# Centring, squares and running sums beside the output projections of a two-layer decoder trunk: their order and their places

## The chip, the cores and the metric

The kernel runs on one core of one Trainium2 chip. The metric is the device time of one execution in microseconds (us). The kernel before took 2110.22 us, the median of 3 runs (2108.76 to 2110.62).

Names used throughout: PE is TensorE with its matmuls, PEld its weight loads, DVE is VectorE, ACT is ScalarE, POOL is GpSimd, SP is SyncE, which issues most DMAs. All operands are 32 bits wide; a matmul operand is split into a high part (a rounding cast, on ACT) and a low part (what the cast left, a subtraction on DVE), and three matmuls (high x high, low x high, high x low) make one product of near full precision.

## The reference, cut to what matters

Two layers over 512 tokens and a width of 2048. Layer 0 mixes by indexed sparse attention, layer 1 by stick-breaking attention; both end in an output projection, and then the same tail:

```python
y = (o * silu(g)) @ w_out                       # output projection, 2048 x 2048
x = layer_norm(DN_ALPHA * x + y, ln_g, ln_b)    # mean and variance over 2048
x = x + (p[i] @ w_ple[i]) * sigmoid(x @ w_ple_gate[i])
```

The kernel holds all activations transposed, as 16 tiles m0 to m15 of 128 features x 512 tokens. The layer norm needs, for each token, the sum and the sum of squares over all 16 tiles.

## The kernel before, in words

**The stream of products.** Everything that PE does is cut into chunks, kept in one list (`chunks`), and `run` issues them in order. A chunk has 512 KB of weights. For chunk c the list of steps issues, ahead of its matmuls: the split of the weights of chunk c+2 (`split_w`: cast wh on ACT, L302, and wl on DVE, L303; there are three buffers of each, so that the split of c+2 needs the end of chunk c-1), sums of two weight tiles on DVE (`add_plus`, L291), accumulating loads issued by POOL (`add_load`, L286) and loads issued by SP (L207, six chunks ahead). Behind the matmuls come the evacuations, whatever was attached to the chunk with `then`, and a `pop`.

**The output projection** (`mix_out`, once a layer). Eight chunks of plain products make m0 to m3 (matmuls over 512 columns, L121 to L123). Then `quads` makes m4 to m15, two at a time, by seven products of half size instead of eight (a Strassen-like scheme; sums and differences of the quarters of u and of the weights are formed beforehand): six sources, each with products P1 to P7. A product is 24 matmuls over 256 columns (L187). The order is P1, P7, P6, P2, P4, P5 for the first source, then for each further one P7, P1, P3 of the source before, P6, P2, P4, P5, and at the very end the last P3. Seven such products are called a period here. The steps of a period: during P5 DVE forms the sum of weights for the next P6 and during P3 that for P4 (L291). After P7, P1, P6 and P3 ACT copies a half result out of PSUM (L217, L221, L225, L250), after P2, P4 and P5 DVE adds two halves (L229, L239, L233; L247 for the last P3). After P4 and after P3 a result tile is complete and goes to `out_done`.

**The layer norm's sums.** `out_done` (L818 on DVE) adds alpha times the residual to a result. When m0 and m1 are there, `guess` makes a rough mean c by one matmul pair; the variance is computed from tiles from which c was subtracted. From then on each tile puts a `center(m)` in a queue (`defer`), and those of m0 to m3 are put there with a due number nine chunks later. `pop` takes one function off this queue if its due number is below the number of the running chunk; a chunk with `pops = 0` takes none. `center` issues four operations: the subtraction of c on DVE (L843), the square on ACT (L850), the add of the tile to a1 on DVE (L851) and the add of the square to a2 on POOL (L852); the first item writes a1 and a2 instead (L846, L847). In the quads, P7, P2 and P5 have `pops = 0`, so pops are at P1, P3, P6 and P4. What is left in the queue after the last product is taken by `finish`, ahead of the matmuls of the first chunk of the per-layer embedding (`ple_chunks`), but behind that chunk's split. After that chunk `ln_stats` has PE sum a1 and a2 over the partitions (L856, L857), and ACT and DVE form mean and variance.

**The forms of u.** `us_ahead(kc)` splits four tiles of u (L105 on ACT, L106 on DVE), which plain chunks (0, kc) and (1, kc) need. `u_sums(j)` forms two differences and two further sums of a pair of u tiles (L770 to L773 on DVE), then splits one of them (L105, L106). It is attached to plain chunks 0 to 6: pairs 0 to 5 to chunks 0 to 5, and pairs 6 and 7 to chunk 6. In layer 1 the last head's attention tail (`b_tail`) hangs on chunks 0 and 2; `us_ahead(2)` hangs on chunk 1 and `us_ahead(3)` on chunk 5, in both layers.

Each engine works off its instructions in the order in which these functions issue them, and waits at an instruction whose inputs are not there.

Of the kernel before, what the change touches and what calls it, by code (L numbers as in the profile page):

```python
# [9 lines left out]
AF = mybir.ActivationFunctionType  # L10
OP = mybir.AluOpType
# [5 lines left out]
KT = D // P  # L17
# [364 lines left out]
def body(tc, xt, pt, positions, lncols, freq, w_in, w_out, w_gate, w_ple, w_kv, w_v, w_q, out):  # L382
    nc = tc.nc
    with tc.tile_pool(name="const", bufs=1) as const, \
            tc.tile_pool(name="raw", bufs=RAW_BUFS) as raw, \
            tc.tile_pool(name="hl", bufs=HL_BUFS) as hl, \
            tc.tile_pool(name="t", bufs=T_BUFS) as tp, \
            tc.tile_pool(name="dram", bufs=1, space=bass.MemoryType.DRAM) as dram, \
            tc.tile_pool(name="psum", bufs=1, space=bass.MemoryType.PSUM) as psum, \
            tc.manual_schedule():  # L390
        k = Kernel(tc, (const, raw, hl, tp, psum, dram))
        _emit(k, xt, pt, positions, lncols, freq, w_in, w_out, w_gate, w_ple, w_kv, w_v, w_q, out)


def _emit(k, xt, pt, positions, lncols, freq, w_in, w_out, w_gate, w_ple, w_kv, w_v, w_q, out):
    nc, const = k.nc, k.const
# [347 lines left out]
    def load_p(layer):  # L744
        pb.clear()
        for f in range(2):
            pb.append(k.tt(s="pin"))
            nc.sync.dma_start(pb[f], pt[layer, f])

    def prep_p(layer):  # L750
        pT[layer] = [k.split(t) for t in pb]

    def us(m):
        if m not in uhl:
            uhl[m] = k.split(u[m][0])
        return uhl[m]

    def us_ahead(kc):
        for m in range(4 * kc, 4 * kc + 4):
            if m in u:  # L760
                us(m)
# [3 lines left out]
    def u_sums(j):  # L765

        us(2 * j), us(2 * j + 1)
        a, b = u[2 * j][0], u[2 * j + 1][0]
        lo, hi = slice(0, HALF), slice(HALF, T)
        nc.vector.tensor_tensor(b[:, hi], b[:, hi], a[:, hi], op=OP.subtract)  # L770
        nc.vector.tensor_tensor(a[:, hi], a[:, lo], a[:, hi], op=OP.subtract)
        nc.vector.scalar_tensor_tensor(a[:, lo], b[:, hi], -1.0, a[:, lo], op0=OP.mult, op1=OP.subtract)
        nc.vector.scalar_tensor_tensor(b[:, lo], a[:, lo], -1.0, b[:, lo], op0=OP.mult, op1=OP.subtract)  # L773
        u23[j] = k.split(a)
        u.pop(2 * j)

    def u_more(name, js):

        for j in js:
            b = u[2 * j + 1][0]  # L780
            if j not in u14:
                u14[j] = k.tt(F32R, "u14")
            t, c = uhl[2 * j][name == "S4"], slice(0, HALF) if name == "S4" else slice(HALF, T)
            nc.scalar.copy(t[:, HALF:], b[:, c])
            nc.vector.tensor_tensor(u14[j][:, c], b[:, c], t.bitcast(F32)[:, HALF:], op=OP.subtract)
            if name == "S4":
                u.pop(2 * j + 1)
# [14 lines left out]
    def u_drop(what):  # L802
        for j in range(KT // 2):
            if what == 0:
                u23.pop(j)
            else:
                uhl.pop(2 * j + (what == 1))
                if what == 2:
                    u14.pop(j)

    dT = {}
    ln = {}
# [3 lines left out]
    def out_done(m, ps, z=None, negated=False):  # L816
        z = k.tt(s="z") if z is None else z
        nc.vector.scalar_tensor_tensor(z, x1.pop(m), ALPHA, ps, op0=OP.mult,  # L818
                                       op1=OP.subtract if negated else OP.add)
        dT[m] = z  # L820
        if len(dT) == 1:
            ln.clear()
        if len(dT) <= 2:
            rough.append(k.tt(F32R, "rough"))
            nc.scalar.copy(rough[-1], z)
        if "c" in ln:
            k.defer(lambda: center(m))
        elif len(dT) == 2:
            k.soon(guess)

    def guess():
        c_ps = k.ps("s")
        for n in range(2):
            nc.tensor.matmul(c_ps, ones_c, rough[n], start=n == 0, stop=n == 1)
        rough.clear()
        ln["c"] = k.tt(s="lnc")
        nc.scalar.copy(ln["c"], c_ps)
        for m in list(dT):
            k.defer_by(9, lambda m=m: center(m))

    def center(m):
        d = dT[m]
        nc.vector.tensor_tensor(d, d, ln["c"], op=OP.subtract)  # L843
        if "a1" not in ln:
            ln["a1"], ln["a2"] = k.tt(s="a1"), k.tt(s="a2")
            nc.vector.tensor_copy(ln["a1"], d)  # L846
            nc.scalar.activation(ln["a2"], d, AF.Square)  # L847
        else:
            sq = k.tt(s="sq")
            nc.scalar.activation(sq, d, AF.Square)  # L850
            nc.vector.tensor_tensor(ln["a1"], ln["a1"], d, op=OP.add)  # L851
            nc.gpsimd.tensor_tensor(ln["a2"], ln["a2"], sq, op=OP.add)  # L852

    def ln_stats():
        m_ps, e_ps = k.ps("s"), k.ps("s")
# [91 lines left out]
    def mix_out(layer):  # L947
        order = [(0, kc) for kc in range(3)] + [(1, kc) for kc in range(3)] + [(0, 3), (1, 3)]
        outs = {}
        for n, (b, kc) in enumerate(order):  # L950
            if b not in outs:
                outs[b] = [Out(KT, lambda ps, m=2 * b + i: out_done(m, ps)) for i in range(2)]
            if n == 0 and layer == 0:
                k.chunks[-3].after = lambda: us_ahead(0)
                k.chunks[-2].after = lambda: us_ahead(1)
            ch = k.chunk4(w_out[layer], 4 * b + kc, kc, outs[b], us,
                          pre=finish if n == 6 and layer == 0 else None)
            k.chunks.append(ch)
            if n in (0, 2) and layer == 1:
                ch.then(lambda n=n: b_tail(HEADS - 1, n // 2))  # L960
            if n in (1, 5):
                ch.then(lambda n=n: us_ahead(2 if n == 1 else 3))
            if kc == 1:
                ch.then(lambda b=b: [x1_load(layer, 2 * b + i) for i in range(2)])
            ch.then(lambda n=n: [u_sums(j) for j in ((6, 7) if n == 6 else (n,) if n < 6 else ())])

        def done(n, which, t):
            out_done(2 * n + 4 + which, t, t, which == 1)

        qs = k.quads([((w_out[layer], 2 * b), (w_out[layer], 2 * b + 1)) for b in range(2, KT // 2)], u_form, done)  # L970
        for n, name in enumerate(("P1", "P7", "P6", "P2")):
            qs[0][name].then(lambda n=n: u_more("S1", (2 * n, 2 * n + 1)))
        for q, name, js in ((0, "P4", (0, 1, 2)), (0, "P5", (3, 4, 5)), (1, "P7", (6, 7))):
            qs[q][name].then(lambda js=js: u_more("S4", js))
        for q in qs:
            for name in ("P7", "P2", "P5"):
                q[name].pops = 0
        for n, q in enumerate(qs):
            q["P7"].then(lambda n=n: x1_load(layer, 2 * n + 4))
            q["P4"].then(lambda n=n: x1_load(layer, 2 * n + 5))  # L980
        last = qs[-1]
        last["P6"].then(lambda: (u_drop(0), load_p(layer)))
        last["P4"].then(lambda: (u_drop(1), prep_p(layer)))
        last["P3"].then(lambda: u_drop(2))

    def x1_load(layer, m):
        x1[m] = k.tt(s="x1")
        nc.sync.dma_start(x1[m], xd[m] if layer else xt[m])
# [48 lines left out]
    def gate_end(n):  # L1037
        for m in range(4 * n, 4 * n + 4):
            xn.pop(m)
        if n < 3:  # L1040
            x1_split(8 + 2 * n)
            x1_split(9 + 2 * n)

    mix_out(0)
    ple_chunks(0)
    gate_block(0, x1_fin)
# [56 lines left out]
    def b_tail(h, step):  # L1103
        a = att[100 + h]
        if h < 4:
            a["v"] = values(vb[0], h)
        tail(h, a)[step]()
        if step == 1:
            if h == 3:
                vb.clear()  # L1110
            if h < KEEP_U:
                k.soon(lambda: u_store(h))
# [13 lines left out]
    qs = k.quads([(where_b[a](ha), where_b[b](hb)) for a, ha, b, hb in plan_b], form, b_done)  # L1126
# [20 lines left out]
    def out_store(m, v):  # L1147
        for c in halves(m):
            nc.sync.dma_start(out[m, :, c], v[:, c])

    mix_out(1)
    ple_chunks(1)
    gate_block(1, out_fin)
# [74 lines left out]
```

## Time and profile before

| | |
|---|---|
| median of 3 runs | 2110.22 us (2108.76 to 2110.62) |
| the profiled execution | 2110.23 us, its span 2108.5 us |
| PE busy | 2083.4 us (99%) |
| PEld busy | 1885.3 us (89%) |
| DVE busy | 1468.8 us (70%) |
| ACT busy | 1029.7 us (49%) |
| POOL busy | 243.7 us (12%) |
| plain chunks and quads of layer 0's projection | to about 792 us of the span |
| the same of layer 1 | about 1732 to 1903 us |

A row of a timeline gives the start within the span and the duration (us), engine, line, operation, output and input tiles, and in brackets how long the engine stood before it and what it waited for. A row of the waits gives the total in us, how often, and the longest. Matmuls overlap: each shows a duration of 0.28 us while the next starts 0.12 us later.

### The profile page before, as it was taken

What the parts mean: (1) busy time and instruction counts of PE and PEld (TensorE: products, weight loads), DVE (VectorE), ACT (ScalarE), POOL (GpSimd) and SP (SyncE); (2) the same over time, 40 slices, a digit from 0 to 9 for tenths busy, and PEclk for the clock granted to TensorE, in tenths of its full rate; (3) what the DMA queues carried; (4) which work ended last, traced back from release to release, by engine and by line L of the source; (5) the groups of instructions that cost most, each with busy time, mean ns of one, the idle gap of its engine ahead of it and who ended that gap; (6) DMA issues with size and microseconds to landing.
All of it is one profiled execution on the core that took longest, in us unless ns stands there. A gap on an engine that the chain in (4) does not pass through costs nothing. (4 is left out here: it accounts for less than half of the span.)

```text
span 2108.5 us, 32807 instructions
## 1 busy us (share of the span) xinstructions
PE 2083.4 (99%) x13024; PEld 1885.3 (89%) x13024; DVE 1468.8 (70%) x2254; ACT 1029.7 (49%) x1645; POOL 243.7 (12%) x311
## 2 busy tenths in 40 slices
PE   9999999999999999999999999999999999999999
PEld 7987888888888997888899999999999998997887
DVE  5577966556578887635777777777777778888633
ACT  4564345445455446423545455545555554446421
POOL 5201000000000220000011111111111110220000
PEclk9999999999999999999999999999999999999999
DMA  6322322222233662433455554655654564563431
GB/s 245 100 100 81 100 81 80 72 79 70 81 110 106 167 187 87 145 110 126 114 132 136 142 157 126 154 147 140 153 158 126 140 216 135 151 186 100 140 120 40
DMA packets 81226, 265.62 MB, mean 126 GB/s; under 512 B 9264, under 2 KB 9520, under 8 KB 81072
## 3 DMA queue, kind: packets, MB, share of 16 engines
q1 hardware_dynamic: 68976, 219.48, 30.6%
q0 software_dynamic: 12096, 44.05, 12.2%
q8 instruction: 102, 1.67, 0.3%
q14 instruction: 52, 0.43, 0.1%
HBM read 251.43 MB, written 12.06 MB: 125 GB/s over the span
## 5 line engine op out<-in xcount | busy, mean ns | idle before, releaser
L303 DVE TENSOR_TENSOR wl<-raw,wh 128x1024 fp32r<-128x1024 f32 (+1 forms) x489 | 607.2, 1246 | 295.0 <-ACT wh L302 290.9
L302 ACT CAST wh<-raw 128x1024 fp32r<-128x1024 f32 (+1 forms) x489 | 509.8, 1048 | 284.2 <-PE g L122 146.2
L187 PE MATMUL g<-f,wh 128*128 128x256 f32 x3360 | 619.4, 284 | 0.0
L121 PE MATMUL g<-h,wh 128*128 128x512 f32 (+1 forms) x1424 | 552.4, 388 | 1.0 <-ACT h L105 1.0
L122 PE MATMUL g<-l,wh 128*128 128x512 f32 (+1 forms) x1424 | 548.0, 385 | 0.8 <-DVE l L106 0.8
L123 PE MATMUL g<-h,wl 128*128 128x512 f32 (+1 forms) x1424 | 547.8, 385 | 0.5 <-DVE wl L303 0.5
L187 PEld LDWEIGHTS g<-f,wh 128*128 128x128 f32 x3360 | 528.6, 192 | 0.8
L187 PE MATMUL g<-f,wl 128*128 128x256 f32 x1680 | 475.5, 283 | 2.2 <-DVE wl L303 2.2
L187 PEld LDWEIGHTS g<-f,wl 128*128 128x128 f32 x1680 | 322.0, 192 | 3.8 <-DVE wl L303 3.0
L121 PEld LDWEIGHTS g<-h,wh 128*128 128x128 f32 x1424 | 267.6, 188 | 55.6 <-issue 2.9
L123 PEld LDWEIGHTS g<-h,wl 128*128 128x128 f32 x1424 | 267.5, 188 | 51.9 <-DVE wl L303 1.0
L122 PEld LDWEIGHTS g<-l,wh 128*128 128x128 f32 x1424 | 267.6, 188 | 51.7 <-DVE l L106 1.2
L187 PE MATMUL g<-h,wl 128*128 128x256 f32 x576 | 164.5, 286 | 8.9 <-DVE wl L303 8.9
L187 PE MATMUL g<-h,wh 128*128 128x256 f32 x576 | 163.1, 283 | 0.0
L187 PE MATMUL g<-l,wh 128*128 128x256 f32 x576 | 161.3, 283 | 0.0
L187 PEld LDWEIGHTS g<-h,wl 128*128 128x128 f32 x576 | 110.4, 192 | 12.0 <-DVE wl L303 11.9
L286 POOL DMA_DIRECT2D raw<-in_w_q_dram x60 | 53.0, 1031 | 585.0 <-issue 241.0
L187 PEld LDWEIGHTS g<-h,wh 128*128 128x128 f32 x576 | 110.4, 192 | 0.3
L187 PEld LDWEIGHTS g<-l,wh 128*128 128x128 f32 x576 | 109.8, 192 | 0.0
L291 DVE TENSOR_TENSOR raw<-raw,raw 128x1024 f32<-128x1024 f32 x84 | 102.3, 1218 | 0.1
L650 ACT ACTIVATE pr<-pr,s 128x128 f32<-128x128 f32 (+1 forms) x64 | 36.1, 564 | 126.0 <-DVE s L649 125.7
L474 POOL TENSOR_TENSOR rb<-rb,sin 128x512 f32<-128x512 f32 (+2 forms) x29 | 35.9, 1240 | 470.2 <-ACT rb L472 292.1
(206 smaller groups left out, 2441.4 us busy)
## 6 DMA issues: line engine op xcount, KB each, us to landing
raw<-in_w_in_dram SPq DMA_DIRECT2D x97, 512.0 KB, 3.3
raw<-in_w_out_dram SPq DMA_DIRECT2D x64, 512.0 KB, 4.2
raw<-in_w_gate_dram SPq DMA_DIRECT2D x64, 512.0 KB, 3.5
raw<-in_w_q_dram SPq DMA_DIRECT2D x64, 512.0 KB, 5.2
raw<-in_w_q_dram POOLq DMA_DIRECT2D x60, 512.0 KB, 6.0
raw<-in_w_kv_dram SPq DMA_DIRECT2D x56, 512.0 KB, 4.1
raw<-in_w_out_dram POOLq DMA_DIRECT2D x24, 512.0 KB, 5.6
xin<-in_x_dram SPq DMA_DIRECT2D x16, 256.0 KB, 6.0
```

The lines of the kernel that those rows point to most:

```text
L121: nc.tensor.matmul(out, ah, bh, start=start, stop=False)
L122: nc.tensor.matmul(out, ah, bl, start=False, stop=False)
L123: nc.tensor.matmul(out, al, bh, start=False, stop=stop)
L187: nc.tensor.matmul(ps[:, :HALF], a, b, start=start and j == 0 and n == 0, stop=stop and j == KT // 2 - 1 and n == 2, skip_group_check=True)
L286: self.nc.gpsimd.dma_start(ch.raw, ch.add, accum_op=OP.add)
L291: self.nc.vector.tensor_tensor(ch.raw, ch.raw, ch.plus.raw, op=OP.add)
L302: nc.scalar.copy(ch.h[:, i:i + w], ch.raw[:, i:i + w])
L303: nc.vector.tensor_tensor(ch.l[:, i:i + w], ch.raw[:, i:i + w], ch.h.bitcast(F32)[:, i:i + w], op=OP.subtract)
L474: nc.gpsimd.tensor_tensor(b[:rows, col:], b[:rows, col:], sin[:rows, col:], op=OP.mult)
L650: nc.scalar.activation(pr[:, :n], pr[:, :n], AF.Exp, bias=mx, scale=1.0, accum_out=sm)
```

## The change

`center` issues only its subtraction, and ahead of it the square and the two adds of the item before (`add_squares`). The last result of the sixteen is not put in the queue: `out_done` takes whatever the queue holds, centres it, and adds its square to a2 on DVE instead of POOL. In the quads of all sources but the last, P2, P4, P5 and P3 have no pops, so that P7, P1 and P6 have one; the products of the last source all have one. In layer 1 `u_sums` is attached one chunk later, with pairs 3 and 4 together on chunk 4.

```diff
@@ out_done
-        if "c" in ln:
+        if len(dT) == KT:
+            k.pop(KT, True)
+            center(m)
+            add_squares(nc.vector)
+        elif "c" in ln:
             k.defer(lambda: center(m))
@@
+    squares = []
+
     def center(m):
-        d = dT[m]
-        nc.vector.tensor_tensor(d, d, ln["c"], op=OP.subtract)
-        if "a1" not in ln:
-            ln["a1"], ln["a2"] = k.tt(s="a1"), k.tt(s="a2")
-            nc.vector.tensor_copy(ln["a1"], d)
-            nc.scalar.activation(ln["a2"], d, AF.Square)
-        else:
-            sq = k.tt(s="sq")
-            nc.scalar.activation(sq, d, AF.Square)
-            nc.vector.tensor_tensor(ln["a1"], ln["a1"], d, op=OP.add)
-            nc.gpsimd.tensor_tensor(ln["a2"], ln["a2"], sq, op=OP.add)
+        add_squares()
+        nc.vector.tensor_tensor(dT[m], dT[m], ln["c"], op=OP.subtract)
+        squares.append(m)
+
+    def add_squares(eng=None):
+        while squares:
+            d = dT[squares.pop()]
+            if "a1" not in ln:
+                ln["a1"], ln["a2"] = k.tt(s="a1"), k.tt(s="a2")
+                nc.vector.tensor_copy(ln["a1"], d)
+                nc.scalar.activation(ln["a2"], d, AF.Square)
+            else:
+                sq = k.tt(s="sq")
+                nc.scalar.activation(sq, d, AF.Square)
+                nc.vector.tensor_tensor(ln["a1"], ln["a1"], d, op=OP.add)
+                (eng or nc.gpsimd).tensor_tensor(ln["a2"], ln["a2"], sq, op=OP.add)
@@ mix_out
+        sums = ({0: (0,), 1: (1,), 2: (2,), 3: (3,), 4: (4,), 5: (5,), 6: (6, 7)},
+                {1: (0,), 2: (1,), 3: (2,), 4: (3, 4), 5: (5,), 6: (6, 7)})
...
-            ch.then(lambda n=n: [u_sums(j) for j in ((6, 7) if n == 6 else (n,) if n < 6 else ())])
+            ch.then(lambda n=n: [u_sums(j) for j in sums[layer].get(n, ())])
...
-        for q in qs:
-            for name in ("P7", "P2", "P5"):
+        for q in qs[:-1]:
+            for name in ("P2", "P4", "P5", "P3"):
                 q[name].pops = 0
```

## Rows read from the trace of the kernel before

**Rows 1.** The page, busy time of the engines.
```profile
PE 2083.4 (99%) x13024; PEld 1885.3 (89%) x13024; DVE 1468.8 (70%) x2254; ACT 1029.7 (49%) x1645; POOL 243.7 (12%) x311
```
**Rows 2.** Waits of PE over the whole span: us, times, longest us.
```profile
PE g L187 <- DVE wl L303: 11.1, 18, 1.2
```
**Rows 3.** Waits of PE in 700 to 770, then in 1800 to 1915 us.
```profile
PE g L187 <- DVE wl L303: 4.2, 7, 1.2
...
PE g L187 <- DVE wl L303: 4.6, 7, 1.2
```
**Rows 4.** Stretches, PE alone: length, busy (matmuls), granted clock, DMA share, GB/s.
```profile
700.00:769.00 69.00, 64.75 (x525) 1.00 0.60 158
1500.00:1569.00 69.00, 69.00 (x569) 1.00 0.57 149
```
**Rows 5.** Timeline of DVE in layer 0's projection.
```profile
744.95 1.21 DVE L303 TENSOR_TENSOR wl<-raw,wh 128x1024 fp32r<-128x1024 f32 x1
746.09 0.41 DVE L239 TENSOR_TENSOR o<-o,g 128x256 f32<-128x256 f32 x1
746.53 0.69 DVE L818 SCALAR_TENSOR_TENSOR o<-x,o 128x512 f32<-128x512 f32 x1
747.14 0.68 DVE L843 TENSOR_TENSOR o<-o,lnc 128x512 f32<-128x512 f32 x1
747.86 0.69 DVE L851 TENSOR_TENSOR a<-a,o 128x512 f32<-128x512 f32 x1
749.54 1.55 DVE L303 TENSOR_TENSOR wl<-raw,wh 128x1024 fp32r<-128x1024 f32 x1 [0.99 <-ACT wh L302]
```
**Rows 6.** Timeline of ACT at the same place.
```profile
747.94 0.63 ACT L850 ACTIVATE sq<-o 128x512 f32<-128x512 f32 x1 [3.88 <-DVE o L843]
748.48 1.98 ACT L302 CAST wh<-raw 128x1024 fp32r<-128x1024 f32 x2
```
**Rows 7.** Timeline of PE at the same place.
```profile
750.49 0.28 PE L187 MATMUL g<-h,wh 128*128 128x256 f32 x1
751.15 0.38 PE L187 MATMUL g<-h,wl 128*128 128x256 f32 x1 [0.38 <-DVE wl L303]
```
**Rows 8.** The page, DMA issues: count, KB each, us to landing.
```profile
raw<-in_w_out_dram POOLq DMA_DIRECT2D x24, 512.0 KB, 5.6
```
**Rows 9.** Timeline of POOL, an add of a square in layer 1.
```profile
1812.94 1.30 POOL L852 TENSOR_TENSOR a<-a,sq 128x512 f32<-128x512 f32 x1 [16.27 <-issue]
```
**Rows 10.** Timeline of DVE at the same place.
```profile
1813.46 1.85 DVE L303 TENSOR_TENSOR wl<-raw,wh 128x1024 fp32r<-128x1024 f32 x1 [0.91 <-ACT wh L302]
```
**Rows 11.** Timeline of DVE at the end of layer 0's projection.
```profile
794.08 0.69 DVE L818 SCALAR_TENSOR_TENSOR o<-x,o 128x512 f32<-128x512 f32 x1
...
797.02 1.54 DVE L303 TENSOR_TENSOR wl<-raw,wh 128x1024 fp32r<-128x1024 f32 x1 [0.92 <-ACT wh L302]
```
**Rows 12.** Timeline of PE at the same place, with the statistics' matmuls.
```profile
797.30 0.39 PE L123 MATMUL g<-h,wl 128*128 128x512 f32 x1
800.03 1.37 PE L856 MATMUL s<-a,ones 128*128 128x512 f32 x2 [2.35 <-DVE a L851]
801.29 2.07 PE L857 MATMUL s<-a,ones 128*128 128x512 f32 x2
```
**Rows 13.** A stretch of the last period: PE, PEld, DVE, ACT, POOL busy (instructions), clock, DMA.
```profile
769.00:792.00 23.00, 23.00 (x194) 23.00 (x193) 18.42 (x22) 11.52 (x17) 3.47 (x3) 1.00 0.67 193
```
**Rows 14.** Timeline of PE, plain chunks 1 and 2 of layer 1's projection.
```profile
1737.63 0.39 PE L123 MATMUL g<-h,wl 128*128 128x512 f32 x1
1739.00 0.50 PE L121 MATMUL g<-h,wh 128*128 128x512 f32 x1 [0.98 <-ACT h L105]
1740.34 0.50 PE L122 MATMUL g<-l,wh 128*128 128x512 f32 x1 [0.84 <-DVE l L106]
```
**Rows 15.** Timeline of ACT at the same place, the cast within u_sums(0).
```profile
1736.86 0.62 ACT L105 CAST h<-u 128x512 fp32r<-128x512 f32 x1 [2.83 <-DVE u L772]
```
**Rows 16.** A stretch after the statistics of layer 0, columns as in rows 13.
```profile
802.00:804.00 2.00, 2.00 (x4) 1.00 (x3) 0.31 (x1) 1.99 (x3) 0.00 (x0) 0.50 0.04 8
```

## The prediction

> **What bounds the kernel now.** I read the page first: PE is busy for 2083.4 of 2108.5 us [rows 1], so all that an edit of the other engines can return is time in which PE stands. The list of PE's waits says for what [rows 2]: above all for the weights' low part wl (L303, on DVE), 18 times. Fourteen of the 18 lie in the two output projections, seven in each [rows 3]. The table of stretches gives the size: 69 us of the first projection hold 525 matmuls of L187, 69 us of the later stage, which has the same kind of products and no centring, hold 569 [rows 4]; the 44 that are missing are 5.3 us at the pitch of 0.12 us.
>
> The timelines of one stall show its cause. DVE centres a result (L843 at 747.14); ACT has stood 3.88 us for that centring, because its queue holds the square (L850 at 747.94) ahead of the next casts of weights (L302 at 748.48) [rows 5, 6]. DVE in turn stands 0.99 us for the cast, forms wl from 749.54 until 751.09, and PE, which took the product's first matmul at 750.49, goes on at 751.15 [rows 5, 7]. DVE and ACT wait for each other in turn.
>
> **The change, part by part.** A product is 24 matmuls at 0.12 us, 2.88 us on PE; a period of seven products is 20.16 us.
>
> *Squares and sums one item late.* Each item keeps its centring, square, a1 add and a2 add; only the last a2 add goes from POOL to DVE. At a pop ACT now squares a tile that was centred a pop before, so its casts no longer stand behind this pop's centring.
>
> *Pops moved.* Before, the pops that may centre lie at P1, P3, P6 and P4; after, at P7, P1 and P6, and in the last period at all seven. P3 and P4 already carry a result each (L818), and P3 a sum of weights. Counting the queue's due numbers by hand: m0 stays at P6 of the second period; then three items go per period (m1 to m9), while two are made. The last period gets m10 (P7), m11 (P1), m12 (P6), m13 (P2) and m14 (P5), then m15 directly; before, it had m12, m13, and m14 and m15 at its very end.
>
> What it is moved past: SP holds none of it. On POOL, the accumulating load for the next P7 is issued in P3; the add of P1's pop now ends some 2.5 us later than the add that stands there today, and the load with it. From issue it lands in 5.6 us [rows 8], just when the cast of P7 comes up, 3 us ahead of what PE needs, so I cost it at nothing; cover is gone if a landing takes over 9 us.
>
> Does DVE have room? Its pitches, start to start [rows 5]: 1.14 us for a 128x1024 operation, 0.44 for a 128x256, 0.61 to 0.72 for a 128x512; I take 0.61, as the two of a pop no longer hang on each other. A period has 7 splits and 2 weight sums (9 x 1.14 = 10.3), 3 small evacuations (1.3), 2 results (1.2) and 3 items (3 x 1.22 = 3.7): 16.5 us. To this comes a cost that hardly shows now. While POOL adds a square, DVE is slowed: wl took 1.55 us instead of 1.21 [rows 5], and where it lay 0.78 us under an add (which ended at 1814.24) 1.85, so 0.64 more [rows 9, 10]. Today DVE idles through the first part of an add; after the change it will work beneath all 1.30 us. Scaled, 0.64/0.78 x 1.30 = 1.07 us an item (an estimate; bounds 0.34, the common case of today, and 1.30, all of the add). Three items: 3.2, in sum 19.7 of 20.16. The Trainium skill, "SBUF — State Buffer", section "Who interferes with whom", says that a VectorE instruction with two SBUF inputs and a GpSimd instruction that reads SBUF contend, the one that comes second being blocked for the whole of the other; by that an item would cost DVE 1.30 and a period 20.4, just over PE's. The overlapped row agrees in kind, at 82% of it.
>
> The fit is tight, but a burst has room: a split is issued two products ahead, 5.76 us, of which cast and split need 2.3. Walking the period by these pitches, DVE is 0.7, 2.3, 2.5 and 2.5 us behind the end of P7, P1, P3 and P6; P2 and P4 have little beside one split and win it back, and every wl is there 2 us before its need. So I take all fourteen stalls as gone. Their price: 4.2 + 4.6 us of idle [rows 3], plus what each loses beside it, since a matmul's 0.28 us counts as busy while the pitch is 0.12 (0.66 from 750.49 to 751.15 instead of 0.12, with 0.38 called idle [rows 7]: 0.16, and some 0.1 in the restart): 8.8 + 14 x 0.26 = 12.4. The counted stretch gives 2 x 5.3 = 10.6. **I take 12.0**, nearer to the timelines, where each start is seen.
>
> *Last result direct.* Before, the last result (L818) begins at 794.08; an older item and a split (797.02) follow on DVE ahead of m15's centring. PE stands for 2.35 us until L856 at 800.03, and L857 comes at 801.29, with POOL's last add [rows 11, 12]. After, m15 goes ahead of that split, but DVE arrives later: three items more before it, 3 x 2.3 = 6.9 us, against the 4.6 of 23 us and what follows in which it stood idle [rows 13]. My walk: wl of the last product is ready 1.0 us before its need, that of the first embedding product 0.5; L818 of m15 ends near 797.3; m14's a1, m15's centring and its a1 take 1.9, so L856 starts near 799.3, and L857 near 800.1, since the a2 add on DVE ends at 800.0. **1.2 us a layer, 2.4 in all**; bounds 0 (DVE a microsecond later) and 4.7 (all of the wait in both). The split put behind m15 is for the third embedding product, more than 5 us off, and costs nothing.
>
> *Layer 1's sums one product back.* At the end of the second product PE goes from 1737.63 to 1739.00 and to 1740.34 where 0.23 each is the pitch, 2.25 us lost [rows 14]. It waits for a split of u that stands on ACT behind the cast of u_sums(0), which itself waited 2.83 us for DVE [rows 15]. Put behind the second product's splits, u_sums(0) lets these begin some 2.5 us sooner. Cover gone elsewhere: sums 3 and 4 now share a product, 5 us of DVE in 5.4, and us_ahead(3) comes 2.8 us nearer to its use, by my walk just in time. **2.2 us**, bounds 1.5 and 2.25.
>
> **Sum.** 12.0 + 2.4 + 2.2 = 16.6. The profiled execution took 2110.23 (span 2108.5 and 1.7 around it), the median is 2110.22. 2110.2 - 16.6 = **2093.6 us**. Not counted: from 802 to 804 the granted clock was 0.50, the lower level (1.2 GHz), after PE's idle 2.35 us [rows 12, 16], 1.0 us lost. I keep it, as PE still stands there, if less.
>
> **Rivals.**
> (a) *DVE fills up.* If an add costs it 1.3 to 1.6 us, a period needs 20.4 to 21.3, DVE falls back by up to 1.1 a period, and over the last periods wl is late again: the 2.4 at the end are lost, and 2 to 3 us a layer in stalls: near 2100. For: 19.7 is already 98% of PE's period. Against: the one row shows 82%, not all, of an overlap. 0.17.
> (b) *Slower: adds and DVE block each other.* POOL's adds now begin amid DVE's work in every period. The old period takes 20.16 and some 1.8 of stalls, 22.0. DVE exceeds it once an add costs (22.0 - 16.5)/3 = 1.8 us. At 2.6, twice an add, a period takes 24.3: 2.3 x 4 periods x 2 layers = 18 us lost, less 2.2 for the sums: about 2126. Against: no row shows over 0.82 of the overlap. 0.04.
> (c) *The end opens fully*: DVE is slowed less (0.34), PE hardly stands at L856, and the clock stays up: 2.3 + 1.0 more, 2090.3. 0.13.
> (d) *It does not do what it says*: DVE runs a product late, so the square still meets a centring not done, as P7 and P1 are only 2.88 us apart; the stalls stay, only the sums return: 2108. For: the walk has DVE 2.5 us late. 0.08.
>
> **How the numbers follow.** Forecast 0.58, (a) 0.17, (b) 0.04, (c) 0.13, (d) 0.08. A measurement of this kernel tells about 0.2% (4.2 us) from no change. Faster by more: forecast, (a) and (c), 0.88; the same: (d), 0.08; slower: (b), 0.04. The range takes in forecast, (a) and (c): its low end is 12.4 + 4.7 + 2.25 and the clock's 1.0 below, 20.4, so 2089.5 with the rounding; its high end is (a) with its larger stalls, 2102.
>
> **What would show it.** Right: PE's waits for wl fall from 18 to the four of the later stage; ACT's square no longer waits for DVE; wl under an add takes up to 2.2 us; a 69 us stretch of the projection holds some 569 matmuls; PE stands 1 to 2 us ahead of L856; no stall at layer 1's start. Wrong: stalls on wl in the last period (a), DVE without idle and PE waiting throughout (b), ACT's square still waiting for L843 (d).

## The result and the profile after

The changed kernel took 2094.5 us, the kernel before 2110.4 beside it: a ratio of 0.9924, 95% interval 0.9905 to 0.9944, so 16 us (12 to 20) faster. One of its four executions took 4157.84 us, twice the time of the others, and is left out as slow. A second set of runs gave 2094.18 us (five runs within 2094.02 and 2094.33) and 0.9922 (0.9909 to 0.9934). The forecast was 2093.6, the range 2089.5 to 2102.0. The profiled execution took 2094.14 us, with a span of 2092.4; the span before was 2108.5.

The page's line of busy times, to be held beside [rows 1]: PE did the same 13024 matmuls in a span that is 16.1 us shorter.

```profile
PE 2079.5 (99%) x13024; PEld 1884.9 (90%) x13024; DVE 1479.1 (71%) x2256; ACT 1026.6 (49%) x1645; POOL 245.1 (12%) x309
```

PE's waits over the whole span, beside [rows 2]. The waits for wl are five instead of 18. Four of the five lie in the later stage, outside the projections; the fifth is new, in the first product of layer 1's quads. New too is a small one for L247, DVE's evacuation of the last product.

```profile
PE s L867 <- DVE a L862: 3.4, 2, 1.7
PE g L187 <- DVE wl L303: 2.1, 5, 0.5
PE o L703 <- POOL ident L400: 1.4, 1, 1.4
PE g L123 <- DVE wl L303: 0.5, 1, 0.5
PE g L121 <- DVE o L247: 0.4, 2, 0.2
```

ACT's waits for the centring ahead of a square, over the whole span: two lines of the kernel before, then one of the changed kernel. 28 such waits are down to four, one in each last period and one ahead of the square of each m15.

```profile
ACT sq L850 <- DVE o L843: 51.1, 22, 3.9
ACT sq L850 <- DVE z L843: 14.1, 6, 3.6
```
```profile
ACT sq L861 <- DVE o L849: 11.7, 4, 4.0
```

Two stretches, all engines, columns as in [rows 13]. The first answers to [rows 4]: 577 matmuls in 69 us instead of 525, with DVE busy for 62.5 of them. The second is the last period, which begins 6 us earlier than before: DVE is busy for 21.7 of 23 us, where it was for 18.4 [rows 13].

```profile
700.00:769.00 69.00, 69.00 (x577) 69.00 (x576) 62.53 (x69) 33.79 (x48) 18.34 (x16) 1.00 0.63 168
763.00:786.00 23.00, 22.98 (x192) 22.78 (x191) 21.71 (x25) 11.45 (x17) 6.43 (x5) 1.00 0.57 171
```

The place that answers to [rows 5 to 7], on DVE, ACT and POOL in turn. The square (now L861) does not wait at all for DVE's centring (now L849), it only follows the copy of PE's result (L221, which stood 0.98 us for PE); the cast comes at 749.49, while DVE is still at the a1 add and the centring ahead of that cast's split. And POOL's add now lies over DVE's work: the centring at 749.82 takes 1.78 us instead of 0.68.

```profile
745.71 0.69 DVE L862 TENSOR_TENSOR a<-a,o 128x512 f32<-128x512 f32 x1
746.31 0.68 DVE L849 TENSOR_TENSOR o<-o,lnc 128x512 f32<-128x512 f32 x1
747.75 1.55 DVE L303 TENSOR_TENSOR wl<-raw,wh 128x1024 fp32r<-128x1024 f32 x1 [0.75 <-ACT wh L302]
749.22 0.68 DVE L862 TENSOR_TENSOR a<-a,o 128x512 f32<-128x512 f32 x1
749.82 1.78 DVE L849 TENSOR_TENSOR o<-o,lnc 128x512 f32<-128x512 f32 x1
```
```profile
748.69 0.38 ACT L221 COPY s<-g 128x256 f32<-128x256 f32 x1 [0.98 <-PE g L187]
748.96 0.64 ACT L861 ACTIVATE sq<-o 128x512 f32<-128x512 f32 x1
749.49 1.04 ACT L302 CAST wh<-raw 128x1024 fp32r<-128x1024 f32 x1
```
```profile
749.74 1.31 POOL L863 TENSOR_TENSOR a<-a,sq 128x512 f32<-128x512 f32 x1 [1.53 <-ACT sq L861]
```

The end of layer 0's projection on PE, beside [rows 12]: PE waits 0.21 us for L247, then 1.72 us ahead of the statistics (L867, L868), where it waited 2.35.

```profile
790.33 0.39 PE L123 MATMUL g<-h,wl 128*128 128x512 f32 x1
790.93 0.50 PE L121 MATMUL g<-h,wh 128*128 128x512 f32 x1 [0.21 <-DVE o L247]
...
792.19 0.40 PE L123 MATMUL g<-h,wl 128*128 128x512 f32 x1
794.31 1.10 PE L867 MATMUL s<-a,ones 128*128 128x512 f32 x2 [1.72 <-DVE a L862]
795.24 1.02 PE L868 MATMUL s<-a,ones 128*128 128x512 f32 x2
```

The same place on DVE, beside [rows 11]. The split that stood ahead of m15 is gone from there, but L247 comes 4 us behind the end of its product, since DVE is late, and L818 takes 1.32 us under POOL's add. Of the 4 us, 0.75 are DVE's wait for a cast. That cast stood on ACT behind a copy of the last source (L236), which had waited 4.80 us for DVE (last line): once, at the end, the two engines still wait for each other in turn.

```profile
788.99 1.55 DVE L303 TENSOR_TENSOR wl<-raw,wh 128x1024 fp32r<-128x1024 f32 x1 [0.75 <-ACT wh L302]
790.47 0.41 DVE L247 TENSOR_TENSOR o<-o,g 128x256 f32<-128x256 f32 x1
790.91 1.32 DVE L818 SCALAR_TENSOR_TENSOR o<-x,o 128x512 f32<-128x512 f32 x1
792.15 0.68 DVE L862 TENSOR_TENSOR a<-a,o 128x512 f32<-128x512 f32 x1
792.76 0.68 DVE L849 TENSOR_TENSOR o<-o,lnc 128x512 f32<-128x512 f32 x1
793.47 0.69 DVE L862 TENSOR_TENSOR a<-a,o 128x512 f32<-128x512 f32 x1
```
```profile
787.12 0.37 ACT L236 COPY o<-g 128x256 f32<-128x256 f32 x1 [4.80 <-DVE o L233]
```

Behind it the granted clock stays at 1.00, where it was 0.50 [rows 16]:

```profile
796.00:798.00 2.00, 2.00 (x10) 1.56 (x9) 0.29 (x1) 1.98 (x4) 0.00 (x0) 1.00 0.31 72
```

Since PE issues the same matmuls in the same order, the two timelines of PE can be laid side by side, matmul by matmul. Each line below is one of them; the difference of two lines is what the stretch between them won or lost.

| matmul | starts before | starts after | shift |
|---|---|---|---|
| layer 0, the first behind the seventh wait | 766.16 | 760.13 | -6.03 |
| layer 0, the last output of the first embedding product | 796.16 | 790.93 | -5.24 |
| layer 0, second statistics matmul | 801.29 | 795.24 | -6.05 |
| layer 0, third matmul after the statistics | 804.01 | 796.56 | -7.45 |
| layer 1, end of plain chunk 1 | 1737.63 | 1729.86 | -7.77 |
| layer 1, chunk 2, second matmul | 1740.34 | 1730.31 | -10.03 |
| layer 1, first product of the quads | 1781.19 | 1771.51 | -9.68 |
| layer 1, the first behind the seventh wait | 1876.93 | 1860.88 | -16.04 |
| layer 1, the last output of the first embedding product | 1906.92 | 1891.68 | -15.24 |
| layer 1, second statistics matmul | 1912.05 | 1895.99 | -16.05 |

Fourteen stalls: 6.03 + 6.36 = 12.4 us won. The last periods: 0.79 + 0.80 lost. The statistics: 0.81 + 0.81 won. The clock of layer 0: 1.40 won. The sums of layer 1: 2.26 won, 0.35 lost again at the first product. The rest, between the layers: 0.3.

### The profile page after: what moved, and what is told of

Read it like the earlier page. It is cut to its first block, busy times and chain, and to the rows that moved or that the text cites. A ratio compares the mean times of both kernels' runs of the same rounds, so it can differ in the third digit from the quotient of the medians.

```text
span 2092.4 us, 32803 instructions
## 1 busy us (share of the span) xinstructions
PE 2079.5 (99%) x13024; PEld 1884.9 (90%) x13024; DVE 1479.1 (71%) x2256; ACT 1026.6 (49%) x1645; POOL 245.1 (12%) x309
## 4 chain that ended last, share of the span: by engine, by line
PE 91%; DVE 4%; issue 3%; ACT 1%; POOL 0%; POOLq 0%; DVEq 0%; ACTq 0%
PE g L187 36%; PE g L121 16%; PE g L123 16%; PE g L122 16%; PE s L592 2%; PE o L122 1%; PE o L123 1%; DVE wl L303 1%; PE o L121 1%; PE s L121 1%; PE s L122 1%; PE s L123 1%; PE s L526 1%; ACT wh L302 1%; DVE a L862 0%
## 5 line engine op out<-in xcount | busy, mean ns | idle before, releaser
L187 PE MATMUL g<-f,wh 128*128 128x256 f32 x3360 | 619.4, 284 | 0.0
L187 PEld LDWEIGHTS g<-f,wh 128*128 128x128 f32 x3360 | 529.1, 192 | 0.8
L187 PE MATMUL g<-f,wl 128*128 128x256 f32 x1680 | 476.3, 284 | 1.9 <-DVE wl L303 1.9
L187 PEld LDWEIGHTS g<-f,wl 128*128 128x128 f32 x1680 | 322.5, 192 | 3.5 <-DVE wl L303 2.7
L187 PE MATMUL g<-h,wl 128*128 128x256 f32 x576 | 163.5, 284 | 0.2 <-DVE wl L303 0.2
L187 PE MATMUL g<-h,wh 128*128 128x256 f32 x576 | 163.3, 284 | 0.0
L187 PE MATMUL g<-l,wh 128*128 128x256 f32 x576 | 161.7, 284 | 0.0
L187 PEld LDWEIGHTS g<-h,wl 128*128 128x128 f32 x576 | 110.7, 192 | 0.7 <-DVE wl L303 0.6
L187 PEld LDWEIGHTS g<-h,wh 128*128 128x128 f32 x576 | 110.7, 192 | 0.1
L187 PEld LDWEIGHTS g<-l,wh 128*128 128x128 f32 x576 | 110.0, 192 | 0.0
L291 DVE TENSOR_TENSOR raw<-raw,raw 128x1024 f32<-128x1024 f32 x84 | 102.4, 1218 | 0.1
```

The source lines that it names most:

```text
L187: nc.tensor.matmul(ps[:, :HALF], a, b, start=start and j == 0 and n == 0, stop=stop and j == KT // 2 - 1 and n == 2, skip_group_check=True)
L291: self.nc.vector.tensor_tensor(ch.raw, ch.raw, ch.plus.raw, op=OP.add)
```

## The experiments

The theory that the result suggests: the stalls are ACT's and DVE's waiting for each other, and DVE's whole work in the last period, POOL's blocking with it, sets when the statistics begin. The rivals stand in each expectation.

**One item late, alone.** The changed kernel with the old pops, the old sums and the last item through the queue, its square issued behind `finish`:

```diff
-        for q in qs[:-1]:
-            for name in ("P2", "P4", "P5", "P3"):
+        for q in qs:
+            for name in ("P7", "P2", "P5"):
```

> Squares and sums one item late; pops, layer 1 sums and the way of the last result as in the kernel before. Theory A (the stalls come from the square that stands on ACT ahead of the casts and waits for this pop's centring): ACT's square waits for DVE almost nowhere, 0 to 4 of the 14 stalls on wl in the projections are left, the time falls by 9 to 12 us against the kernel before, to 2098 to 2101. Theory B (the stalls come from items put on P3 and P4, which already carry a result and a sum of weights, so that DVE itself is late): 10 or more of the 14 are left and the time falls by less than 3 us. Under both the 2.2 us at the start of layer 1 stay.

Measured: 2103.9 us, ratio 0.9975 (0.9965 to 0.9984). Neither theory's number: in the side-by-side, 4.1 of layer 0's 6.0 us come back and 4.4 of layer 1's 6.4, but three of the seven stalls of each layer are left, with waits of 0.3 to 0.5 us. The square still waits for DVE there, 1.59 us at 737.83, and the timeline of DVE says why: the item is put on P3, behind a weight sum (L291) and a result (L818) that an add of POOL (last line) stretches to 1.78 us, and the next pop's square meets a centring that is not done.

```profile
737.83 0.63 ACT L857 ACTIVATE sq<-o 128x512 f32<-128x512 f32 x1 [1.59 <-DVE o L845]
```
```profile
733.61 1.21 DVE L291 TENSOR_TENSOR raw<-raw,raw 128x1024 f32<-128x1024 f32 x1
734.75 1.78 DVE L818 SCALAR_TENSOR_TENSOR o<-x,o 128x512 f32<-128x512 f32 x1
736.45 0.68 DVE L858 TENSOR_TENSOR a<-a,o 128x512 f32<-128x512 f32 x1
737.05 0.68 DVE L845 TENSOR_TENSOR o<-o,lnc 128x512 f32<-128x512 f32 x1
```
```profile
733.70 2.28 POOL L859 TENSOR_TENSOR a<-a,sq 128x512 f32<-128x512 f32 x1 [0.27 <-ACT sq L857]
```

That is rival (d) of the prediction in part: it comes true, at other products than it named, as long as the pops stay where they were.

**Pops moved, alone.** The kernel before, with

```diff
-        for q in qs:
-            for name in ("P7", "P2", "P5"):
+        for q in qs[:-1]:
+            for name in ("P2", "P4", "P5", "P3"):
```

> Pops moved to P7, P1 and P6 (all seven in the last period); square behind its own centring, sums and last result as before. Theory A: the square still waits for its centring on ACT, 8 or more of the 14 stalls are left, the time falls by less than 5 us against the kernel before. Theory B: 0 to 4 of the 14 stalls are left and the time falls by 9 to 12 us. Walking one period by the row's pitches, P1's and P6's squares would each hold ACT about 1 us and yet every wl would be in time, which is theory B's result; the last period, with five items, would show stalls of its own.

Measured: 2108.5 us, ratio 0.9989 (0.9979 to 0.9998), hardly anything. Up to the sixth stall layer 0 wins 4.0 us, then gives 3.6 back: with five items in the last period the stalls come there. In 700 to 769 us PE waits twice for wl, 1.4 us in all, and in 769 to 800 us, by the waits of that stretch:

```profile
PE g L187 <- DVE wl L303: 1.7, 2, 1.0
PE s L856 <- DVE a L851: 1.6, 1, 1.6
PE g L121 <- DVE o L247: 0.5, 1, 0.5
```

By the time this is theory A's result; by the stalls up to the last period, where two of seven are left in each layer, it is nearer to theory B's.

By the medians the two parts are worth 5.3 and 0.8 us alone and, with the sums, 10.3 together (below), but these times mix levels of the clock. In the first experiment's profile the granted clock fell behind both layers' statistics, and no execution's mean clock was above 0.998; of the kernel before beside it, six executions of 25 have 0.998. Against those six (median 2112.2 us) the first experiment's six at 0.998 (median 2103.5) are 8.7 us faster, about what its stalls show (4.1 + 4.4). The pops with the mean clock at 1.000 (two executions, 2107.0, against 2109.1) are worth 2.1, the sums 2.0 (next experiment), and the kernel with all three at 0.999 (2098.9 against 2110.7) 11.8. So the late square is the dearest of the parts, and together they are worth no more than their sum. Light places keep DVE's lateness short enough that an item is centred when the next pop's square comes; the late square keeps ACT free. That is how the traces above read.

**Layer 1's sums, alone.** The kernel before, with the table of sums of the change:

```diff
-            ch.then(lambda n=n: [u_sums(j) for j in ((6, 7) if n == 6 else (n,) if n < 6 else ())])
+            ch.then(lambda n=n: [u_sums(j) for j in sums[layer].get(n, ())])
```

> Only the layer 1 sums one product back; all else as before. The step's own price by the two traces: 2.26 us won at the start of layer 1, 0.38 us given back as a stall on wl in the first product of the quads, so 1.9 us net: 2108.3 to 2108.6. If the 0.38 belongs to the centring and not to the sums, it is absent here and 2.2 to 2.3 us are won.

Measured: 2110.05 us, ratio 1.0000 (0.9990 to 1.0009), not the time that was expected. The side-by-side shows the step's price as expected: 2.26 us won, 0.39 lost at the first product, so that loss belongs to the sums and not to the centring. But it did not reach the end: in this execution the granted clock fell behind layer 1's statistics too, which it had not in the profile of the kernel before, and 1.6 us went there. Nine of the ten executions have a mean clock of 0.998 (median 2110.2); against the six of the kernel before at that clock (2112.2) the sums return 2.0 us. These are stretches of PE alone, columns as in [rows 4]:

```profile
1910.00:1912.00 2.00, 1.85 (x5) 0.90 0.53 207
1912.00:1914.00 2.00, 2.00 (x5) 0.50 0.00 0
1914.00:1916.00 2.00, 2.00 (x8) 0.74 0.00 0
```

**All but the direct last result.** The changed kernel, m15 through the queue and its add on POOL:

```diff
-        if len(dT) == KT:
-            k.pop(KT, True)
-            center(m)
-            add_squares(nc.vector)
-        elif "c" in ln:
+        if "c" in ln:
...
-            ch = Chunk(k.whole(w_ple[layer], c), mms, pre=finish if c == 0 else None)
+            ch = Chunk(k.whole(w_ple[layer], c), mms, pre=(lambda: (finish(), add_squares())) if c == 0 else None)
```

> The changed kernel, but the last result goes through the queue and is centred behind the first embedding product's split, its a2 add on POOL. If taking the last result directly is worth what the traces show of L856 and L857 (0.8 us a layer and the clock of layer 0, 1.4 us, that goes with the shorter wait), the time is 1.6 to 3.5 us above the changed kernel, 2096 to 2098, and PE stands over 2.3 us ahead of the statistics. Rival: the end is set by DVE's whole work in the last period, in whatever order, and the time stays within 0.5 us of the changed kernel's.

Measured: 2098.9 us, ratio 0.9945 (0.9931 to 0.9960), against 0.9922 for the changed kernel: 4.8 us by the spans (2097.2 against 2092.4), more than was expected, and the rival is out. The list of PE's waits has up to 3.0 us ahead of the statistics, more than in the kernel before, and layer 0's clock falls again. In layer 1, where it does not fall, the difference is 1.7 us:

```profile
PE s L863 <- DVE a L858: 6.1, 2, 3.0
```

**The direct last result, alone.** The kernel before, with these lines, where the second argument puts the last a2 add on DVE:

```diff
-        if "c" in ln:
+        if len(dT) == KT:
+            k.pop(KT, True)
+            center(m, nc.vector)
+        elif "c" in ln:
             k.defer(lambda: center(m))
```

> The kernel before with the last result centred directly and its square added on DVE, all else as before. Ahead of the statistics a split (1.5 us under POOL's add) and 0.9 us of waiting for its cast go: L856 comes 1.5 to 2.4 us sooner a layer, 3 to 5 us in all and up to 3 us more where the lower clock behind the wait is avoided: 2102 to 2106. If instead taking it directly is only worth something beside the five items of the moved last period, the time falls by less than 2 us.

Measured: 2104.35 us against 2110.29, ratio 0.9971 (0.9960 to 0.9983): 5.9 us. By the side-by-side 1.8 us a layer of it are won at the statistics, and 1.4 are layer 0's clock. By the list of PE's waits the one ahead of the statistics is down to 0.9 us, and all 18 for wl are still there; the clock stays up in the profiled execution.

```profile
PE g L187 <- DVE wl L303: 10.4, 18, 1.2
PE s L859 <- DVE a L854: 1.7, 2, 0.9
```

**The changed kernel again**, without an edit, as the measure for the next.

> The changed kernel once more, beside the three below on the same chip. By its first runs 2094 to 2095 us. Some executions may be about 1.5 us longer: in the kernel before and in three of the experiments the granted clock fell to the lower level behind the wait ahead of the statistics of one layer or of both, and their times lie in steps of that size.

Measured: 2094.18 us; no run above 2094.33, no step.

**All adds of squares on DVE.** They are made one pop after their square, so that DVE does not wait for ACT.

```diff
-    squares = []
+    squares, sums_due = [], []
...
     def add_squares(eng=None):
+        while sums_due:
+            nc.vector.tensor_tensor(ln["a2"], ln["a2"], sums_due.pop(), op=OP.add)
...
-                (eng or nc.gpsimd).tensor_tensor(ln["a2"], ln["a2"], sq, op=OP.add)
+                sums_due.append(sq)
+        if eng:
+            add_squares()
```

> The changed kernel with all adds of squares on DVE, each one pop after its square, so that POOL adds nothing. Theory (an add on POOL costs DVE 1.10 us, as a1 shows with 1.78 instead of 0.68 us): an item costs DVE 0.61 for the add instead of 1.10, some 0.5 us less an item and 0.6 less on the last result; DVE ends the last period some 2.4 us sooner, the stall on the last evacuation goes and PE's wait ahead of the statistics falls from 1.7 to below 0.5 us: 2089.5 to 2091.5. Rival (what slows DVE is not POOL's add, or DVE's lateness does not set the end): DVE has 0.61 us more an item, PE waits longer ahead of the statistics, 2095 to 2098.

Measured: 2091.4 us, ratio 0.9909 (0.9895 to 0.9922), 2.8 us less than the changed kernel. The operation behind an add on DVE starts 0.60 us after it, and no other is stretched; the stall on L247 is gone. PE's longest wait ahead of the statistics is 1.3 us, not the 0.5 that was expected: the direction is the theory's, but the wait fell by 0.4 of the 1.2 us, as PE itself comes there 1.1 us sooner. First the timeline of DVE, then a line of PE's waits:

```profile
778.60 0.68 DVE L854 TENSOR_TENSOR a<-a,sq 128x512 f32<-128x512 f32 x1
779.20 0.68 DVE L864 TENSOR_TENSOR a<-a,o 128x512 f32<-128x512 f32 x1
779.80 0.68 DVE L849 TENSOR_TENSOR o<-o,lnc 128x512 f32<-128x512 f32 x1
```
```profile
PE s L871 <- DVE a L864: 2.7, 2, 1.3
```

**That, and a pop at P2 in every period.**

```diff
-            for name in ("P2", "P4", "P5", "P3"):
+            for name in ("P4", "P5", "P3"):
```

> All adds of squares on DVE as in the experiment before, and a pop at P2 in every period, so that the queue is empty sooner and the last period has three items (m12 at P7, m13 at P6, m14 at P5) instead of five. Theory (DVE's work in the last period sets when the statistics begin): two items of 1.83 us less there, more than the 1.3 us that PE still stands ahead of the statistics; PE hardly waits there and 2.4 us go: 2088.5 to 2089.5. Rival (the chain from the last product through its evacuation, centring and square sets it): the wait stays above 0.9 us and the time within 0.8 us of 2091.4. A second or third period with four items needs 20.1 of 20.16 us of DVE and may show a stall or two of 0.3 us.

Measured: **2088.99 us**, ratio 0.9899 (0.9885 to 0.9912): the fastest kernel of the study, 5.2 us below the changed one. PE does not wait for the statistics at all any more, and no stall on wl is left in layer 0's projection, so the rival is out; DVE's idle time is back in the last period (19.5 of 23 us busy, columns as in [rows 13]):

```profile
763.00:786.00 23.00, 23.00 (x194) 23.00 (x194) 19.52 (x26) 12.17 (x18) 0.86 (x1) 1.00 0.74 238
```

**The pop at P2 with the adds on POOL**, by the same edit of the changed kernel.

> The changed kernel, adds on POOL, with a pop at P2 in every period. By the same theory two items of 2.3 us less in the last period: the 0.8 us of stalls there and most of the 1.7 us wait go in each layer, up to 5 us, but the third period now has four items, 12.8 + 4 x 2.3 = 22 of 20.16 us, and stalls on wl of 1 to 2 us a layer come there: 2090 to 2093. Rival as above: 2093.5 to 2095.

Measured: 2092.9 us, ratio 0.9917 (0.9903 to 0.9930). The wait ahead of the statistics is gone here too, but PE's list has six more stalls on wl. In layer 0 they lie between 734 and 746 us, where a period now has four items under POOL's blocking:

```profile
PE g L187 <- DVE wl L303: 4.1, 11, 0.5
```

By the side-by-side layer 0 loses some 2 us there and wins 2.7 at its end. With the adds on DVE the same pops lose nothing there. That tells the two causes apart: too many items at the end, and the price of an item.

**Filling PE's wait**, eight transposes in the changed kernel, sixteen in the kernel before, both ahead of `ln_stats`:

```diff
-                ch.after = ln_stats
+                ch.after = lambda: (warm(8), ln_stats())
```

> The changed kernel with eight transposes of the identity on PE ahead of the statistics' matmuls, where PE stands for 1.7 us. Theory (the lower clock after the statistics comes from PE's standing there): no execution shows the lower level there, and the times no longer lie in steps; the median stays within 0.5 us of the changed kernel's, as its profiled execution had no such fall. Rival (the statistics' own matmuls, whose operands are not split, bring the fall): it comes as often as before.

> The kernel before with sixteen transposes of the identity on PE ahead of the statistics' matmuls, where PE stands 2.35 us; at 0.11 us each, as the experiment with eight showed, they fill some 1.8 us of it. Theory (the lower clock comes from PE's standing there): the granted clock stays at the upper level behind both layers' statistics, the times gather at the low end of the kernel before, 2108 to 2109, and none lies above 2110.5, while the kernel before beside it keeps its steps from 2108.5 to 2112.5. Rival (the statistics' own matmuls bring it, or nothing near it): the steps stay as they are beside it.

Measured: 2094.13 us, the same as the changed kernel, which has no fall of the clock to lose; and 2109.15 against 2110.45 for the kernel before, ratio 0.9997 (0.9988 to 1.0006). Of eleven runs of the filled kernel none lies above 2110.41, where the kernel before beside it reaches 2112.03; seven lie below 2109.4, four near 2110.35. The highest step is gone and a lower one is left, which points to PE's standing still as part of the cause; that it is all of it is not shown, and the interval allows no claim on the median.

## Why the prediction was right, and where it was not

**The stalls.** 12.0 us were taken, 12.4 measured; the timelines' count, where each start is seen, was the better of the two. The other count was low because of a misread stretch: of the 569 matmuls in the later stage [rows 4] only some 510 are L187, and among the others are matmuls over 512 columns that start up to 0.24 us apart. The changed kernel's own stretch holds 577. That all fourteen would go held. The reason held too: the square left ACT's way, by the list of ACT's waits and by the timeline above. What the text did not say is that neither of its two parts would do it alone; the walk was made with both.

**What an item costs.** What an add of POOL costs DVE, estimated at 1.07 us from one overlapped row, is 1.10 (1.78 instead of 0.68) seven times in layer 0's projection, and less where part of the add meets idle time. DVE's sum of 98% of a period was right in kind: 62.5 of 69 us busy, no stall, and a fourth item stalls it (the pop at P2). But scaling the row in proportion was right in size only: the loss is the time for which the operation lies under the add, less 0.13 to 0.14 us (0.78 gave 0.64 [rows 9, 10], 1.23 gives 1.10 at 749.82). The rule of the Trainium skill, "SBUF — State Buffer", section "Who interferes with whom", has whichever of the two comes second blocked for the whole of the other. The traces agree with it up to these 0.13 us or so; taken as 1.30 for every add it would have given 20.4 us a period and rival (a), and the measured 1.10 decides. POOL's add was itself drawn out where DVE came first, to 1.45 us in places and 2.06 at the end.

**The end.** Here a step failed: "1.2 us a layer, 2.4 in all" was nearly nothing, 0.81 won at the statistics and 0.80 lost before them. The walk through the last period came out 1 us too early: wl of the last product was to be ready 1.0 us before its need and was late (0.18 us lost), and L818 was stretched by 0.63. It also missed a wait: the last output of the first embedding product needs the PSUM tile that L247 evacuates, and L247 stood behind DVE's lateness (0.38 and some after). Behind this the step mixed two things that the experiments part: taking the last result directly is worth about 5 us (5.9 alone, 4.8 on top), of which some 1.4 are the clock, and what is left, 1.7 to 1.8 us a layer, is taken back by the three further items in the last period.

**The sums.** 2.2 predicted, 1.9 measured: 2.26 won as counted, and 0.35 to 0.39 lost at the first product of the quads, where the walk had looked only as far as us_ahead(3).

**The clock.** Kept at the lower level in the forecast, it stayed up: 1.4 us that were named (as 1.0) and not counted. So 2093.6 against 2094.1 is partly luck: 2.4 too much at the end, 0.3 too much for the sums, against 0.4 too little for the stalls, 1.4 for the clock and 0.3 between the layers.

**The rivals.** (a) is there in small, two stalls a layer of 0.2 to 0.4 us; (b) fell, as no add costs DVE more than 1.13 in layer 0; (c) needs the adds off POOL or fewer items at the end; (d) is in part what the old pops do.

## What to carry to other kernels

Where two engines hand work to each other in one order, an instruction that waits for its own pop's result holds everything behind it on its engine: issue it one step later, and check that the place where its input is made is not itself late. When a queue is thinned in the middle, count what piles up at its end, where nothing hides it. An add moved to POOL is not free for DVE: here it cost DVE 0.34 us where DVE stood idle at its start, 1.10 where DVE worked through it, and 0.60 on DVE itself, so that it is a loss once DVE is full. And before times of single parts are added up, look whether the clock was at the same level in them.

## What the runs showed of the hardware that was not expected

A DVE operation with both inputs in SBUF that starts under an add of POOL loses the rest of that add, less 0.13 to 0.14 us: 0.34 us for 0.47 under it, 0.63 for 0.77 (L818 at 790.91), 0.64 for 0.78 [rows 9, 10], 1.10 for 1.23 (the centring at 749.82). It goes the other way too: an add that starts while such an operation runs is drawn out by a little less than what is left of that, to 2.28 us behind L291 in the first experiment and, in the line below, to 2.06 behind the split at 788.99. Where DVE's second input is in PSUM, as with L247 at 790.47, it keeps its 0.41 us under the same add:

```profile
789.62 2.06 POOL L863 TENSOR_TENSOR a<-a,sq 128x512 f32<-128x512 f32 x1 [0.16 <-ACT sq L861]
```

The granted clock falls to the lower level behind the statistics in some executions and layers and not in others, at 1.4 to 1.7 us a time: in layer 0 alone of the kernel before's profile, in both layers of the first experiment and the third, in layer 1 alone of the second, where PE had waited just 1.6 us, in layer 0 alone of the fourth, where PE waited 3.0 us in both, and in neither profile of the changed kernel, with 1.7. So the length of the wait alone does not decide it. The kernel before scatters over 2108.3 to 2112.9 us in this study, the changed one over 2094.0 to 2094.5. What decides it beyond PE's standing still stays open.
